# Trainium2, one core: a lightning indexer emitted in portions of half a projection, each held on TensorE behind that half

## The chip, the cores and the metric

The kernel runs on one core of a Trainium2 chip. The time is device microseconds of one execution, and the figure compared is the median of several executions. TensorE is called PE below, VectorE DVE, ScalarE ACT, GpSimd POOL, and SyncE, which issues the DMAs here, SP.

## What is computed

Two layers of a decoder trunk over 1024 tokens of width 1024, all in float32. Each layer normalises its input, multiplies it with one wide matrix, and runs two branches over the result: a sparse attention, whose keys are picked by an indexer, and a gated DeltaNet. The two branches are gated, added and multiplied with an output matrix. What matters here is the indexer and the choice of keys:

```python
raw = jnp.einsum('bqhd,bsd->bqhs', qib, k_idx)              # 8 index heads of width 64
iscore = jnp.einsum('bqhs,bqh->bqs', jax.nn.relu(raw), wb)  # one score per query and key
iscore = jnp.where(causal[None], iscore, -jnp.inf)
_, sel = lax.top_k(iscore, topk)                            # topk = 256 keys per query
```

Tokens come in eight blocks of 128 (`t` = 0 to 7). Blocks 0 and 1 see at most 256 keys, so only the blocks 2 to 7 (`SEL`) need scores and a choice.

## The kernel before, in words

Products in full precision are made of three matmuls: each operand is split into a high part (written by ACT, line 139) and a low part (DVE, line 140). A **projection** is 8 steps of k with three matmuls each, 24 in all, of 512 columns; `proj_tokens` (line 338) makes one per token block, `proj_feat` (line 361) one per half of 512 tokens.

A layer runs through `token_phase`, `feature_phase` and `attention`. The change is in `token_phase`. There the PE makes, in this order: the projections of the index columns (`first`, `second`); 24 projections of queries, keys and values (three chunks `ch` of eight blocks each); and 16 projections of the attention gates (`gate_a`, four features of four projections). With those 40 projections it shares its time with a generator, `self.beside`. This generator first gives the indexer (`index_scores`), and then the choice of keys (`select`, in two stages that alternate). After each projection `tick()` takes pieces out of the generator until their costs have used up `SHARE` = 4.0. What a piece emits stands in program order behind that projection. The framework's scheduler then makes a fixed queue for each engine, with program order as priority and with waits where data are needed; an instruction that it takes for ready may move ahead of one that isn't.

One **unit** of the indexer is a pair of index heads of one block: 6 or 12 matmuls of 64 rows (line 511) into the four banks `wide`, their relu on ACT (line 513) and two weighted additions into `scores` on DVE (lines 518 and 520). A unit costs `2 * n / S`, where n is the block's number of keys: 0.75 for block 2 up to 2.0 for block 7. There are four units per block, 24 in a layer. A block's queries are turned just ahead of its first unit: four PE transposes (line 498), then a split by ACT and DVE into `qi_hi` and `qi_lo`. Line 523 masks a block's finished scores.

`select` searches the 256th largest score of each query bit by bit: 31 iterations in each stage, one piece of cost `SEL_COST` = 1.5 each. Stage 0 has the blocks 5 (counted on DVE, line 544) and 4, 3, 2 (counted on ACT with Sign, line 562); stage 1 has block 7 on DVE and block 6 on ACT. Both stages share one buffer for DVE's count (`t_junk`) and one for ACT's (`t_junk2`), so their pieces follow each other. After the search come two corrective counts, and then a mask for each of six blocks (lines 607 to 613), which SP writes out (line 614).

When the phase ends its tiles are freed, and `feature_phase` takes their space: `xp` (line 682), `xf` (line 644) and the decay rows `H` (line 665). Projections of the first DeltaNet head can run ahead of that, since their results wait in PSUM; `acc` has two banks and `more` one, so three of them fit. Lines 687 and 688 move them into `xp` and `kf`.

SP holds one queue in order: the loads of weights (`w_raw`, line 303), the writing of masks (line 614), of staged tokens (line 387) and of gates (line 636) all pass through it.

Of the kernel before, what the change touches and what calls it, by code (L numbers as in the profile page):

```python
# [37 lines left out]
S = 1024  # L38
D = 1024
T = S // P  # L40
KT = D // P
# [13 lines left out]
SEL = list(range(TOPK // P, T))  # L55

SEL_STAGES = [([5], [4, 3, 2]), ([7], [6])]

SHARE, SEL_COST = 4.0, 1.5

GATES = (4, 2, 1, 1)

# [24 lines left out]
class Trunk:  # L87
    def __init__(self, ctx, tc, args):
        self.tc, self.nc = tc, tc.nc
        (self.x, self.positions, self.norm_gain, self.w_in, self.conv_w, self.a_log, self.dt_bias,  # L90
         self.gdn_gain, self.idx_gain, self.w_out, self.final_gain, self.out) = args
        self.depth = self.w_in.shape[0]
        self.const = ctx.enter_context(tc.tile_pool(name="const", bufs=1))
        self.dram = ctx.enter_context(tc.tile_pool(name="scratch", bufs=1, space=DRAM))
        self.act = ctx.enter_context(tc.tile_pool(name="act", bufs=1))
        self.small = ctx.enter_context(tc.tile_pool(name="small", bufs=2))
        self.wp = ctx.enter_context(tc.tile_pool(name="bulk", bufs=1))
        self.tags, self.turn = {}, 0
        self.beside = None
        ctx.enter_context(self.banks(acc=(1, 2), tr=(1, 2)))  # L100


# [178 lines left out]
                self.split(ht[0][:, ks, ts], ht[1][:, ks, ts], pt.rearrange("p (k t) -> p k t", k=4))  # L281
        return ht

    def tick(self):

        left = SHARE
        while left > 0 and self.beside is not None:
            cost = next(self.beside, None)
            if cost is None:
                self.beside = None  # L290
            else:
                left -= cost


    def w_tiles(self, srcs, n):
# [28 lines left out]
    def proj_tokens(self, weights, act, evac, t0=0, tag=lambda t: "acc", then=None):  # L324


        nc = self.nc
        ws, n, _ = weights
        order = [(t, k) for t in range(t0, T) for k in range(KT)]
        if then:  # L330
            order.sort(key=lambda x: (x[0], x[1]) if x[0] < T - 2 else (T - 2, x[1] + LAG * (x[0] == T - 1)))
        acc = {}
        for t, k in order:
            if t not in acc:
                acc[t] = self.bank(tag(t))
            ts = slice(t * P, (t + 1) * P)
            for i, (a, b) in enumerate(((act[0], 0), (act[0], 1), (act[1], 0))):
                nc.tensor.matmul(acc[t][:, :n], a[:, k, ts], ws[k][b][:, :n], start=k == 0 and i == 0,  # L338
                                 stop=k == KT - 1 and i == 2)
            if then and t == T - 1:  # L340
                then[0].append(next(then[2]))
            if k == KT - 1:
                evac(t, acc.pop(t)[:, :n])
                self.tick()

    def feat_weights(self, w, c0):

# [6 lines left out]
    def proj_feat(self, ws, half, act, evac, tag="acc"):  # L354

        hs = slice(half * 512, half * 512 + 512)
        acc = self.bank(tag)
        for k in range(KT):
            cs = slice((k % 4) * P, (k % 4 + 1) * P)
            for i, (a, b) in enumerate(((0, 0), (0, 1), (1, 0))):  # L360
                self.nc.tensor.matmul(acc, ws[k // 4][a][:, cs], act[b][:, k, hs], start=k == 0 and i == 0,  # L361
                                      stop=k == KT - 1 and i == 2)
        evac(hs, acc)
        self.tick()


    def token_phase(self, l, ip, ht, first):
# [92 lines left out]
    def index_scores(self, l, p, raw, scores):  # L460
        nc = self.nc
        shape = [P, T, 8]
        wi = self.small.tile(shape, F32, name="w_idx", bufs=1)
        nc.vector.tensor_scalar(wi, raw[:, :, 576:584], IDXH ** -0.5 * IDXD ** -0.5, None, op0=OP.mult)

        kn2 = p.tile([P, T, 2, IDXD], F32, name="relu", bufs=3)
        kn = kn2[:, :, 0]
        sq = p.tile([P, T, IDXD], F32, name="relu", bufs=3)
        kr = raw[:, :, 512:576]
        nc.vector.tensor_mul(sq, kr, kr)  # L470
        ssq = self.small.tile([P, T], F32, name="k_ssq")
        nc.vector.tensor_reduce(ssq, sq, axis=AX.X, op=OP.add)
        nc.vector.tensor_scalar(ssq, ssq, 1.0 / IDXD, EPS, op0=OP.mult, op1=OP.add)
        r = self.rsqrt(ssq, T)
        kshape = [P, T, IDXD]
        nc.vector.tensor_mul(kn, kr, r[:, :, None].to_broadcast(kshape))
        nc.vector.tensor_mul(kn, kn, self.ig[l][:, None, :].to_broadcast(kshape))
        self.rope(p, kn2[:, :, 0:1], slice(0, T), self.rope_i, 1)
        nc.scalar.copy(kn2[:, :, 1], kn)
        kh = p.tile([P, S], F32R, name="k_hi")  # L480
        kl = p.tile([P, S], F32R, name="k_lo")
        for half in range(2):
            pt = self.tr()
            for i in range(4):
                nc.tensor.transpose(pt[:, i * P:(i + 1) * P], kn2[:, 4 * half + i].rearrange("p a d -> p (a d)"),
                                    self.ident)
            hs = slice(512 * half, 512 * half + 512)
            self.split(kh[:, hs], kl[:, hs], pt)

        t0 = SEL[0]  # L490
        q4 = raw[:, t0:, 0:512].rearrange("p t (h d) -> p t h d", d=IDXD)
        self.rope(p, q4, slice(t0, T), self.rope_i, IDXH)
        for t in SEL:

            qh, ql = (p.tile([P, IDXH // 2, P], F32R, name=nm, bufs=2) for nm in ("qi_hi", "qi_lo"))
            pt = self.tr()
            for i in range(IDXH // 2):
                nc.tensor.transpose(pt[:, i * P:(i + 1) * P], raw[:, t, i * P:(i + 1) * P], self.ident)
            self.split(*(a.rearrange("p h t -> p (h t)") for a in (qh, ql)), pt)
            n = (t + 1) * P  # L500
            sc = scores[t]
            parts = 1 if n <= 512 else 2
            w = n // parts
            for i in range(IDXH // 2):
                rel = [p.tile([P, S], F32, name="relu", bufs=3) for _ in range(2)]
                for o in range(0, n, w):
                    ps = [self.bank("wide") for _ in range(2)]
                    for j, (a, b) in enumerate(((qh, kh), (qh, kl), (ql, kh))):
                        for half in range(2):
                            rows = slice(IDXD * half, IDXD * half + IDXD)  # L510
                            nc.tensor.matmul(ps[half][:, :w], a[rows, i], b[rows, o:o + w], start=j == 0, stop=j == 2)
                    for half in range(2):
                        nc.scalar.activation(rel[half][:, o:o + w], ps[half][:, :w], AF.Relu)
                for half in range(2):
                    h = 2 * i + half
                    wc = wi[:, t, h:h + 1]
                    if h == 0:
                        nc.vector.tensor_scalar(sc[:, :n], rel[half][:, :n], wc, 0.0, op0=OP.mult, op1=OP.add)
                    else:
                        nc.vector.scalar_tensor_tensor(sc[:, :n], rel[half][:, :n], wc, sc[:, :n], op0=OP.mult,  # L520
                                                       op1=OP.add)
                yield 2 * n / S
            nc.vector.tensor_tensor(sc[:, n - P:n], sc[:, n - P:n], self.causal_sel, op=OP.min)


# [620 lines left out]
```

## Time and profile before

| | us |
|---|---|
| median of three executions | 2730.17 (2725.91 to 2731.36) |
| the profiled execution, its own time | 2725.06 |
| its span from the first to the last instruction | 2723.3 |
| its mean granted TensorE clock | 0.976 of 2.4 GHz |

The profile is of one execution. Its span is 1.8 us shorter than its time, and its time lies 5.1 us under the median. "Busy" counts the time in which an engine worked on instructions. Behind each idle time stands the instruction that ended last before the engine could go on. The two layers run the same instructions: the index units stand at 86 to 168 us in the first layer and at 1432 to 1514 us in the second.

### The profile page before, as it was taken

How to read it: one execution, taken by the hardware profiler on the slowest of the kernel's cores; microseconds unless marked ns; L12 is line 12 of the kernel's file. 1: busy time of each engine (PE TensorE's matmuls, PEld its weight loads, DVE VectorE, ACT ScalarE, POOL GpSimd, SP SyncE). 2: the span in 40 equal slices, each digit the busy share in tenths (PEclk: the TensorE clock that was granted, in tenths of full speed). 3: DMA queues.
4: the chain of work that ended last, by engine and by line, in shares of the span. 5: the costliest groups of instructions: out<-in, count | busy, mean ns of one | idle time of the engine just before them, and what ended most of it. 6: DMA issues, size and time to landing. Idle time of an engine off the chain costs nothing.

```text
span 2723.3 us, 42939 instructions
## 1 busy us (share of the span) xinstructions
PE 2570.7 (94%) x14854; PEld 2140.5 (79%) x14854; DVE 1972.8 (72%) x5450; ACT 1316.8 (48%) x3169; POOL 111.9 (4%) x398
## 2 busy tenths in 40 slices
PE   7999989999999999999999999898999999999998
PEld 7677778777777888898786777686887778888986
DVE  6677967767787775697366888677676777757965
ACT  5579643343333332697245894433333343227962
POOL 0122000000000000000001210000000000000000
PEclk9999999999999999999999999998899999999999
DMA  3113332222222221531420232321212221226324
GB/s 121 48 66 90 85 87 56 49 51 57 61 51 53 50 73 51 174 105 35 157 65 30 78 101 71 77 63 47 53 42 65 51 57 46 69 63 180 92 68 143
DMA packets 283262, 202.95 MB, mean 75 GB/s; under 512 B 55906, under 2 KB 241188, under 8 KB 283044
## 3 DMA queue, kind: packets, MB, share of 16 engines
q1 hardware_dynamic: 283044, 200.20, 26.2%
q8 instruction: 117, 1.92, 0.3%
q14 instruction: 101, 0.83, 0.1%
HBM read 153.80 MB, written 46.33 MB: 73 GB/s over the span
## 4 chain that ended last, share of the span: by engine, by line
PE 68%; DVE 13%; ACT 7%; DMA 6%; issue 5%; POOL 1%; SPq 0%; DVEq 0%; POOLq 0%; ACTq 0%
PE acc L361 20%; PE acc L338 11%; PE more L361 9%; PE acc L1038 4%; PE wide L1006 4%; PE tr L758 2%; PE tr L1029 2%; ACT t_junk L562 2%; PE out L338 2%; ACT g_junk L723 2%; DMA w_raw<-in_w_in_dram 2%; DVE t_junk L544 2%; DVE w_lo L140 2%; DMA H<-rows 2%; PE tr L708 1%
## 5 line engine op out<-in xcount | busy, mean ns | idle before, releaser
L361 PE MATMUL acc<-hi_t,w_hi 128*128 128x512 f32 x1240 | 502.2, 405 | 8.3 <-DVE gate L629 7.3
L361 PE MATMUL acc<-hi_t,w_lo 128*128 128x512 f32 x1240 | 501.9, 405 | 0.0
L361 PE MATMUL acc<-lo_t,w_hi 128*128 128x512 f32 x1240 | 499.6, 403 | 0.0
L139 ACT CAST w_hi<-w_raw 128x512 fp32r<-128x512 f32 (+1 forms) x336 | 201.1, 602 | 371.0 <-PE acc L361 196.8
L140 DVE TENSOR_TENSOR w_lo<-w_raw,w_hi 128x512 fp32r<-128x512 f32 (+1 forms) x336 | 223.3, 668 | 149.2 <-ACT w_hi L139 136.0
L338 PE MATMUL acc<-w_hi,hi_t 128*128 128x512 f32 (+1 forms) x768 | 285.7, 373 | 12.6 <-ACT w_hi L139 7.3
L338 PE MATMUL acc<-w_lo,hi_t 128*128 128x512 f32 (+1 forms) x768 | 284.5, 371 | 2.1 <-DVE w_lo L140 1.9
L338 PE MATMUL acc<-w_hi,lo_t 128*128 128x512 f32 (+1 forms) x768 | 283.6, 369 | 0.0
L361 PEld LDWEIGHTS acc<-hi_t,w_hi 128*128 128x128 f32 x1240 | 236.7, 191 | 49.8 <-DVE gate L629 8.6
L361 PEld LDWEIGHTS acc<-hi_t,w_lo 128*128 128x128 f32 x1240 | 236.2, 190 | 41.1
L361 PEld LDWEIGHTS acc<-lo_t,w_hi 128*128 128x128 f32 x1240 | 236.3, 191 | 40.9
L562 ACT ACTIVATE t_junk<-scores,t_bits 128x640 f16<-128x640 f32 x248 | 198.8, 802 | 30.8 <-DVE t_bits L554 26.0
L361 PE MATMUL more<-hi_t,w_hi 128*128 128x512 f32 x488 | 198.8, 407 | 4.5 <-ACT kf L688 4.5
L361 PE MATMUL more<-hi_t,w_lo 128*128 128x512 f32 x488 | 199.2, 408 | 0.0
L361 PE MATMUL more<-lo_t,w_hi 128*128 128x512 f32 x488 | 198.3, 406 | 0.0
L338 PEld LDWEIGHTS acc<-w_hi,hi_t 128*128 128x128 f32 x768 | 146.2, 191 | 40.6 <-ACT w_hi L139 10.5
L338 PEld LDWEIGHTS acc<-w_lo,hi_t 128*128 128x128 f32 x768 | 146.7, 191 | 27.4 <-DVE w_lo L140 5.1
L338 PEld LDWEIGHTS acc<-w_hi,lo_t 128*128 128x128 f32 x768 | 146.6, 191 | 22.0 <-issue 1.0
L544 DVE TENSOR_SCALAR_CACHE_REDUCE t_junk<-scores,t_bits 128x1024 f16<-128x1024 f32 (+4 forms) x136 | 153.4, 1128 | 4.3
L849 DVE TENSOR_TENSOR xc<-xc,xtmp 128x248 f32<-128x248 f32 (+30 forms) x496 | 141.8, 286 | 3.1
L847 DVE TENSOR_TENSOR xtmp<-wide,xc 128x248 f32<-128x248 f32 (+30 forms) x496 | 141.6, 285 | 2.7
L806 ACT ACTIVATE o_junk<-vb 128x128 f32<-128x128 f32 x128 | 39.6, 310 | 162.3 <-DVE vb L803 126.3
(344 smaller groups left out, 5478.4 us busy)
## 6 DMA issues: line engine op xcount, KB each, us to landing
w_raw<-in_w_in_dram SPq DMA_DIRECT2D x272, 256.0 KB
qs<-stage SPq DMA_DIRECT2D x32, 256.0 KB
ya_gate<-gate SPq DMA_DIRECT2D x32, 256.0 KB
H<-rows SPq DMA_DIRECT2D x16, 512.0 KB
wide<-hscr SPq DMA_DIRECT2D x64, 128.0 KB
yb<-gate SPq DMA_DIRECT2D x32, 256.0 KB
w_raw<-in_w_out_dram SPq DMA_DIRECT2D x32, 256.0 KB
qraw<-qs SPq DMA_DIRECT2D x32, 256.0 KB
```

Source lines behind the costliest of these rows:

```text
L139: self.nc.scalar.copy(hi, src)
L140: self.nc.vector.tensor_sub(lo, src, hi.bitcast(F32))
L338: nc.tensor.matmul(acc[t][:, :n], a[:, k, ts], ws[k][b][:, :n], start=k == 0 and i == 0, stop=k == KT - 1 and i == 2)
L361: self.nc.tensor.matmul(acc, ws[k // 4][a][:, cs], act[b][:, k, hs], start=k == 0 and i == 0, stop=k == KT - 1 and i == 2)
L544: nc.vector.tensor_scalar(junk[:, :sc[i].shape[1]], sc[i], thr, 0.0, op0=op, op1=OP.add, accum_out=cnt[:, i:i + 1])
L562: nc.scalar.activation(junk[:, :n], sc[i], AF.Sign, bias=f(bits, i), scale=-1.0, accum_out=cnt[:, i:i + 1])
L723: nc.scalar.activation(junk, pt[:, c * P:(c + 1) * P], AF.Square, accum_out=ssq[:, col:col + 1])
L758: nc.tensor.matmul(pg[:, o0:o0 + P], kf[:, cs], a[:, cs], start=True, stop=True)
L847: nc.vector.tensor_mul(tmp[:, :, j + 1:], ln[:, None, j, j + 1:].to_broadcast(shape), X[:, :, j:j + 1].to_broadcast(shape))
L849: nc.vector.tensor_add(X[:, :, j + 1:], X[:, :, j + 1:], tmp[:, :, j + 1:])
L1006: nc.tensor.matmul(ps[:, :w], qt[a][:, i], kt[b][:, g, o:o + w], start=j == 0, stop=j == 2)
L1038: nc.tensor.matmul(po, a, b[:, cs], start=j == 0 and i == 0, stop=j == t and i == 2)
```

## The change

`tick` takes the matmul behind which the new work has to stand (`mm`), and is called twice in each projection, after the fourth and after the eighth step of k (`proj_feat` likewise). A call adds `SHARE` = 2.0 to a credit that is carried from call to call, and takes pieces while the credit is above zero. What is emitted stands inside `issue_after(mm.ins)`: an instruction on PE may not move ahead of that matmul. Other engines are not held. The cost of a unit is multiplied by `SCORE_COST` = 1.5, the preparation of the keys with the first queries becomes a piece of cost 1.5 of its own, and a piece of `select` costs 1.4 in place of 1.5. The queries of the next block are turned behind the second unit of a block, so two units ahead of their use; the first block's are turned in the piece of the preparation.

```diff
-SHARE, SEL_COST = 4.0, 1.5
+SHARE, SCORE_COST, SEL_COST = 2.0, 1.5, 1.4
...
-    def tick(self):
-
-        left = SHARE
-        while left > 0 and self.beside is not None:
-            cost = next(self.beside, None)
-            if cost is None:
-                self.beside = None
-            else:
-                left -= cost
+    def tick(self, mm):
+
+        if self.beside is None:
+            return
+        self.credit += SHARE
+        with self.tc.issue_after(mm.ins):
+            while self.credit > 0 and self.beside is not None:
+                cost = next(self.beside, None)
+                if cost is None:
+                    self.beside, self.credit = None, 0.0
+                else:
+                    self.credit -= cost
...
             if k == KT - 1:
                 evac(t, acc.pop(t)[:, :n])
-                self.tick()
+            if k % 4 == 3:
+                self.tick(mm)
...
+            if k == KT // 2 - 1:
+                self.tick(mm)
         evac(hs, acc)
-        self.tick()
+        self.tick(mm)
...
-        for t in SEL:
+
+        def queries(t):
...
             self.split(*(a.rearrange("p h t -> p (h t)") for a in (qh, ql)), pt)
+            return qh, ql
+
+        later = queries(t0)
+        yield SCORE_COST
+        for t in SEL:
+            qh, ql = later
...
-                yield 2 * n / S
+                if i == 1 and t + 1 < T:
+                    later = queries(t + 1)
+                yield SCORE_COST * 2 * n / S
```

## Rows read from the trace of the kernel before

**Rows 1.** The page: busy us, share of the span and instructions of each engine.
```profile
PE 2570.7 (94%) x14854; PEld 2140.5 (79%) x14854; DVE 1972.8 (72%) x5450; ACT 1316.8 (48%) x3169; POOL 111.9 (4%) x398
```
**Rows 2.** Waits of PE, 83 to 168 us: us, times, longest; last row 1429 to 1514.
```profile
PE wide L511 <- ACT qi_hi L139: 3.9, 4, 2.7
PE wide L511 <- ACT relu L513: 1.1, 3, 0.5
PE wide L511 <- DVE qi_lo L140: 0.7, 2, 0.4
...
PE wide L511 <- ACT qi_hi L139: 3.6, 4, 2.3
```
**Rows 3.** Hand-over: timeline of ACT and PE at 374 us, then in the second layer.
```profile
374.47 0.59 ACT L687 COPY xp<-acc 128x512 f32<-128x512 f32 x1 [4.81 <-DMA mask<-t_junk]
375.70 0.50 PE L361 MATMUL acc<-hi_t,w_hi 128*128 128x512 f32 x1 [1.04 <-ACT kf L688]
...
1721.06 0.58 ACT L687 COPY xp<-more 128x512 f32<-128x512 f32 x1 [7.13 <-DMA mask<-t_junk]
1722.29 0.50 PE L361 MATMUL more<-hi_t,w_hi 128*128 128x512 f32 x1 [3.35 <-ACT kf L688]
```
**Rows 4.** Line 361 alone: stretch and length, PE busy (count), PEld, clock, DMA, GB/s.
```profile
265.30:374.70 109.40, 105.70 (x456) 86.38 (x455) 0.98 0.33 92
```
**Rows 5.** Timeline of DVE (first row) and ACT about the search's start.
```profile
173.36 0.41 DVE L523 TENSOR_TENSOR scores<-scores,causal_sel 128x128 f32<-128x128 f32 x1
...
137.39 0.61 ACT L562 ACTIVATE t_junk<-scores,t_bits 128x384 f16<-128x384 f32 x1
...
177.68 1.04 ACT L562 ACTIVATE t_junk<-scores,t_bits 128x896 f16<-128x896 f32 x1 [6.58 <-DVE t_bits L554]
```
**Rows 6.** Stretches: length, PE busy, PEld, DVE, ACT, POOL (counts), clock, DMA, GB/s.
```profile
83.20:167.60 84.40, 78.21 (x433) 55.92 (x431) 53.63 (x78) 48.48 (x104) 13.04 (x42) 0.98 0.13 44
177.70:313.00 135.30, 130.72 (x561) 107.06 (x560) 113.20 (x342) 128.42 (x290) 25.31 (x96) 0.97 0.29 85
313.00:374.50 61.50, 57.84 (x247) 46.85 (x245) 50.54 (x109) 10.63 (x19) 0.00 (x0) 0.97 0.27 78
```
**Rows 7.** Line 511 on PE in each layer: minimum/median/maximum ns, first and last start.
```profile
L511 PEld LDWEIGHTS wide<-k_hi,qi_hi x80: 182/183/328, 86.6 to 166.6; 64*128 64x128 f32 x80
...
L511 PEld LDWEIGHTS wide<-k_hi,qi_hi x80: 182/183/326, 1432.8 to 1512.6; 64*128 64x128 f32 x80
```
**Rows 8.** Line 338 alone in three stretches; columns as in rows 4.
```profile
76.80:83.30 6.50, 5.99 (x24) 4.35 (x24) 1.00 0.55 137
...
83.30:167.50 84.20, 39.49 (x160) 29.01 (x159) 0.98 0.13 43
167.60:204.50 36.90, 36.90 (x162) 30.25 (x162) 1.00 0.19 65
```
**Rows 9.** A group of ACT, 177.68 to 313 us: count, busy, mean ns, idle before.
```profile
L562 ACT ACTIVATE t_junk<-scores,t_bits 128x896 f16<-128x896 f32 (+1 forms) x121 | 97.3, 804 | 8.9 <-DVE t_bits L554 6.6
```
**Rows 10.** Groups of DVE, 313 to 374.5 us; a second gate group equals the one shown.
```profile
L140 DVE TENSOR_TENSOR w_lo<-w_raw,w_hi 128x512 fp32r<-128x512 f32 x10 | 6.8, 681 | 0.0
...
L607 DVE TENSOR_SCALAR t_junk<-scores,t_bits 128x768 f16<-128x768 f32 (+5 forms) x6 | 3.5, 586 | 9.1 <-DMA mask<-t_junk 9.1
L629 DVE SCALAR_TENSOR_TENSOR gate<-th,acc 128x512 f32<-128x512 f32 x4 | 2.7, 680 | 0.0
```
**Rows 11.** Timeline of PE after a long wait.
```profile
405.24 1.11 PE L708 MATMUL tr<-ident,qf 128*128 128x128 f32 x4 [7.27 <-DVE kdec L713]
...
409.42 0.64 PE L361 MATMUL acc<-hi_t,w_hi 128*128 128x512 f32 x1
409.90 0.40 PE L361 MATMUL acc<-lo_t,w_hi 128*128 128x512 f32 x1
```
**Rows 12.** Timeline of ACT and PE where a load of weights came late.
```profile
332.24 0.62 ACT L139 CAST w_hi<-w_raw 128x512 fp32r<-128x512 f32 x1 [3.81 <-DMA w_raw<-in_w_in_dram]
...
334.35 0.53 PE L361 MATMUL acc<-hi_t,w_hi 128*128 128x512 f32 x1 [3.63 <-DVE gate L629]
```

More of the change, by code (lines that the diff above doesn't have):

```diff
@@ L282, in make_h @@
         return ht
-    def tick(self):
-        left = SHARE
-        while left > 0 and self.beside is not None:
-            cost = next(self.beside, None)
-            if cost is None:
-                self.beside = None
-            else:
-                left -= cost
+    def tick(self, mm):
[6 more added lines that the diff above has]
+                if cost is None:
+                    self.beside, self.credit = None, 0.0
+                else:
+                    self.credit -= cost
     def w_tiles(self, srcs, n):
@@ L337, in proj_tokens @@
             for i, (a, b) in enumerate(((act[0], 0), (act[0], 1), (act[1], 0))):
-                nc.tensor.matmul(acc[t][:, :n], a[:, k, ts], ws[k][b][:, :n], start=k == 0 and i == 0,
-                                 stop=k == KT - 1 and i == 2)
+                mm = nc.tensor.matmul(acc[t][:, :n], a[:, k, ts], ws[k][b][:, :n], start=k == 0 and i == 0,
+                                      stop=k == KT - 1 and i == 2)
             if then and t == T - 1:
@@ L360, in proj_feat @@
             for i, (a, b) in enumerate(((0, 0), (0, 1), (1, 0))):
-                self.nc.tensor.matmul(acc, ws[k // 4][a][:, cs], act[b][:, k, hs], start=k == 0 and i == 0,
-                                      stop=k == KT - 1 and i == 2)
+                mm = self.nc.tensor.matmul(acc, ws[k // 4][a][:, cs], act[b][:, k, hs], start=k == 0 and i == 0,
+                                           stop=k == KT - 1 and i == 2)
+            if k == KT // 2 - 1:
+                self.tick(mm)
         evac(hs, acc)
-        self.tick()
+        self.tick(mm)
     def token_phase(self, l, ip, ht, first):
```

## The prediction, made before the changed kernel was run

> **What bounds the kernel now.** I read the shares of the page first, then the waits of PE, then the places where PE waits, each in the view that shows who is late there. PE is busy 94% of the span [rows 1], so the first guess is that PE is the bound and that each wait taken from it shortens the kernel. In the stretch of the indexer these waits are small: 3.9 us on the split of the queries, 1.1 us on relu and 0.7 us on the low part, 5.7 us in the first layer; the second repeats the two small ones and has 3.6 us in the large, 5.4 us together [rows 2].
>
> The place that decides lies 207 us later. At 374.5 us ACT, idle for 4.81 us, starts on line 687 when the last mask has been written, because `xp` takes space that `select` held; PE goes on 1.2 us later, after 1.04 us of waiting. In the second layer the same pair waits 7.13 and 3.35 us [rows 3]. By then PE has made 456 matmuls of line 361, which is 19 projections: the 16 gates and the three that fit into free banks [rows 4]. So PE is out of work when the choice of keys ends, in both layers. From there back, the end of `select` sets the time, and PE has no slack to give.
>
> What sets the end of `select`? Its first Signs run at 134.8 to 138 us, one iteration of stage 0, and then none until 177.68 us [rows 5]: the stages alternate through shared buffers, so stage 0 cannot go on before stage 1 has begun, and stage 1 needs the scores of block 7, which line 523 finishes at 173.8 us. From 177.7 to 313 us ACT is busy 128.4 of 135.3 us: the search runs at ACT's pace. Then DVE makes masks for 61.5 us [rows 6]. The chain from the last index unit to the hand-over is stiff: its last group of matmuls starts at 166.6 and 1512.6 us [rows 7], `xp` at 374.47 and 1721.06 us, so 207.9 and 208.5 us, though PE waits 2.3 us longer in the second layer [rows 3].
>
> **The change part by part**, for one layer.
>
> *Where the last unit stands.* By the old costs the first tick gives five units, then 4, 4, 3, 3, 3 and 2: the 24th is out after seven projections. The seventh and eighth blocks of a chunk are made alternately (a lag of two steps of k), so five steps of the eighth stand ahead of it too: 7 x 24 + 15 = 183 matmuls. The trace shows 24 and 160 of line 338 up to there [rows 8], so the scheduler did follow program order. By the new costs a layer's indexer costs 1.5 + 1.5 x 33 = 51, and 2.0 come in per half projection. Adding it up piece by piece, the last unit comes out at the 25th call, after the first half of the 13th projection (block 4 of the second chunk): 300 matmuls. It cannot move ahead, because it is held. That is 117 matmuls of 36.9 / 162 = 0.228 us [rows 8] ahead of it that stood behind it: **+26.7 us** until the last scores. PE's total work is unchanged, but these projections no longer cover the search.
>
> *The waits of the indexer.* Queries turned two units ahead hide their split (on ACT and DVE) behind a whole unit and half a projection, and a unit per half projection gives ACT time for its relu. I let 5.5 us of 5.7 and 5.4 go [rows 2]: **-5.5 us**. Ends: -5.7, and -3 if the new spacing makes small waits of its own. If that cover were lost, the old waits would return and nothing more.
>
> *The backlog behind the last unit.* Before, the last call emits two units, and scores are finished 6 to 7 us after the last group starts (166.6 to 173.8 us) [rows 5, 7]. After it is one unit: **-2.2 us**, ends 0 and -2.6.
>
> *The search.* The 121 Signs in its stretch [rows 9] are the same, and PE makes about as many projections beside it, so ACT has about as many copies: **0**, ends -3 and +3. Emitting it at 1.4 moves its pieces behind later projections in program order, but it already ran later than emitted: the last iterations come out behind projection 29 of 40 before and 35 after, and by 313 us PE was at projection 32.
>
> *The masks.* In the 61.5 us DVE also does 10 splits (6.8 us) and 8 gate steps (twice 2.7 us), 12.2 us in all, some of it inside the 9.1 us for which it waits on the masks' DMAs [rows 10]. PE will be further ahead by then, with fewer evacuations left: **-4 us**, ends 0 and -12. The masks' DMAs move with them in SP's queue (a rival, below).
>
> *The restart.* PE will be idle for some 20 us where it waited 1 to 3. After 7.27 us idle its matmuls took 0.64 us until 409.9 us, then 0.40 [rows 11]: 4.7 us at what the durations show as the lower of its two clock levels (1.2 GHz), 2.3 us lost. Most of it falls into the next wait, that same 7.27 us: **+0.5 us**, ends 0 and +2.3.
>
> *At no cost.* The hold itself: units stood behind their projections before. On the ticks that carry only `select` it holds nothing, since `select` has no PE instruction. No unit issues a DMA.
>
> Sum: 26.7 - 5.5 - 2.2 + 0 - 4 + 0.5 = **+15.5 us per layer, +31 us for two**. Cross-check: PE's 207 us from the indexer's end to the hand-over lose 26.7 us of work, so PE arrives near 369 us or earlier, and the hand-over falls to about 390 us. The profiled execution took 2725.1 us, so 2756 us for its like; it lies 5.1 us under the median, and with the median of 2730.2 I say **2761 us**.
>
> **The rivals.**
>
> *Faster: PE is the bound after all.* The Trainium skill, "Perfetto Trace Analysis", § Identifying the Most-Contended Engine and § Optimization Strategy, says to optimise the engine with the highest occupancy first, and to close the gaps on it; the 94% of the profile's page agree with its choice of engine. As a mechanism here: spread over more projections the indexer leaves ACT free (35.9 of 84.4 us were free before [rows 6]), stage 0's Signs run there ahead of stage 1, the search ends no later than now, and only the 10.9 us of waits change: 2719 us. Three Signs of stage 0 at 0.804 us [rows 9] are 2.4 us per iteration, so the 15.5 us are won back with the seventh iteration run ahead; from there on it isn't slower. Against it stand the 40 us without a Sign [rows 5], and the code that makes the stages alternate is not changed. Chance 0.07.
>
> *Slower still: weights behind masks.* SP's queue is in order. Before, PE lost 3.63 us where a split waited 3.81 us on a late load [rows 12]. If the loads of the first head's weights come to stand behind masks that are now written later, the three projections that ran ahead run after the hand-over: 3 x 24 x 0.23 = 16.6 us per layer, 2761 + 33 = 2794 us. Against it: the loads ran between the masks before, and the three projections were done in time [rows 4]. Chance 0.09.
>
> *No change to speak of:* the change doesn't do what it says, because portions come out later but DVE and ACT take the gain and the loss in equal parts (waits -5.5 and masks -12, search -3, against 26.7 less the backlog): 2730 to 2737 us. Chance 0.04.
>
> **How the numbers follow.** Forecast 0.80, the three rivals 0.07, 0.09 and 0.04. The predicted time is 2761 us. All low ends at once give 26.7 - 5.7 - 2.6 - 3 - 12 = +3.4 us per layer (2737 us), all high ends 26.7 - 3 + 3 + 2.3 = +29 us (2788 us); neither is likely whole. I take 2742 to 2788 us. About 0.2% (5.5 us) is what a measurement can tell from no change: faster 0.07, the same 0.04, slower 0.89.
>
> **What would show it.** Right: the last group of line 511 starts some 19 to 21 us later after the indexer's start, with 300 projection matmuls ahead of it; the waits on `qi_hi` are gone; line 523 ends for block 7 near 192 us; ACT is full for about 135 us from there; and line 687 starts near 390 us with PE idle for some 20 us before it. Wrong, if Signs of stage 0 run in a row before block 7 has scores, if PE reaches line 687's wait with no idle time, or if the search takes clearly less than 135 us. PE idle ahead of the 19th projection with ACT waiting on `w_raw` would be the slower rival.

## The result and the profile after

| | before | after |
|---|---|---|
| median, us | 2728.86 (4 executions) | 2756.43 (4 executions, 2751.51 to 2757.67) |
| profiled execution: time, us | 2725.06 | 2756.95 |
| its span, us | 2723.3 | 2755.2 |
| mean granted TensorE clock | 0.976 | 0.969 |

The changed kernel takes 1.0098 of the time of the one before (95% interval 1.0081 to 1.0116), 27.6 us more. The forecast was +31 us. In the rows below some lines have moved: 338 is 341 now, 361 is 365, 511 is 524, 562 is 577, 607 is 622, 629 is 644, and 687 and 688 are 702 and 703.

The page's first row shows that every engine runs as many instructions as in [rows 1], and that PE is 12.8 us less busy, in a span that is 31.9 us longer:

```profile
PE 2557.9 (93%) x14854; PEld 2132.1 (77%) x14854; DVE 1973.9 (72%) x5450; ACT 1313.6 (48%) x3169; POOL 119.6 (4%) x398
```

The waits of PE, longest first (us in total, times, longest), show where the time is. Behind the first, which was 47.9 us before, stand two new ones, on the hand-over. The last row is the only wait of PE from 83 to 184 us: those of the indexer in [rows 2] are gone.

```profile
PE tr L840 <- DVE vb L836: 49.8, 10, 6.0
PE more L365 <- ACT kf L703: 35.5, 2, 33.9
PE acc L365 <- ACT kf L703: 31.8, 1, 31.8
...
PE tr L505 <- DVE idx_raw L259: 0.8, 1, 0.8
```

The hand-over itself, in the timelines of ACT and PE, first layer and second, answers to [rows 3]. ACT and PE both stand still until the last mask is written:

```profile
386.95 0.59 ACT L702 COPY xp<-acc 128x512 f32<-128x512 f32 x1 [35.53 <-DMA mask<-t_junk]
388.18 0.80 PE L365 MATMUL acc<-hi_t,w_hi 128*128 128x512 f32 x1 [31.75 <-ACT kf L703]
...
1751.85 0.59 ACT L702 COPY xp<-more 128x512 f32<-128x512 f32 x1 [37.66 <-DMA mask<-t_junk]
1753.08 0.79 PE L365 MATMUL more<-hi_t,w_hi 128*128 128x512 f32 x1 [33.88 <-ACT kf L703]
```

The stretches that answer to [rows 6] (length, then busy time and count of PE, PEld, DVE, ACT and POOL, granted clock, DMA share, GB/s): the indexer, the search, the masks. The indexer now runs with PE full and the clock at its upper level, and the search still takes 135 us at ACT's pace. In the masks' stretch PE has 28.7 us of work where it had 57.8, none of it behind 356.4 us, and the granted clock is 0.79, a mean over its two levels:

```profile
86.30:183.20 96.90, 96.77 (x531) 71.94 (x531) 55.74 (x78) 49.96 (x109) 24.38 (x67) 1.00 0.17 55
191.00:326.00 135.00, 131.27 (x575) 107.09 (x574) 118.01 (x351) 129.83 (x294) 17.50 (x66) 1.00 0.31 88
326.00:387.00 61.00, 28.70 (x126) 23.09 (x124) 45.54 (x100) 5.38 (x11) 0.01 (x1) 0.79 0.18 53
```

How far back the last unit stands is read from the projection's matmuls ahead of it: line 341 alone from the first projection to the last unit (columns as in rows 4; answers to [rows 8]), then the first and last start of line 524 in the two layers (answers to [rows 7]), and the first Sign behind the scores (answers to [rows 5]). It is 300 matmuls, and the last group starts 95.7 us after the first, where that was 80.0 us:

```profile
76.80:181.50 104.70, 74.22 (x300) 54.71 (x300) 1.00 0.20 61
...
L524 PEld LDWEIGHTS wide<-k_hi,qi_hi x80: 182/183/187, 86.4 to 182.1; 64*128 64x128 f32 x80
...
L524 PEld LDWEIGHTS wide<-k_hi,qi_hi x80: 182/183/187, 1450.3 to 1546.0; 64*128 64x128 f32 x80
...
190.99 1.04 ACT L577 ACTIVATE t_junk<-scores,t_bits 128x896 f16<-128x896 f32 x1 [4.24 <-DVE t_bits L569]
```

### The profile page after: what moved, and what is told of

The parts are those of the page before. It is cut to its first block, busy times and chain, and to the rows that moved or that the text cites. A ratio compares the mean times of both kernels' runs of the same rounds, so it can differ in the third digit from the quotient of the medians.

```text
span 2755.2 us, 42933 instructions
## 1 busy us (share of the span) xinstructions
PE 2557.9 (93%) x14854; PEld 2132.1 (77%) x14854; DVE 1973.9 (72%) x5450; ACT 1313.6 (48%) x3169; POOL 119.6 (4%) x398
## 4 chain that ended last, share of the span: by engine, by line
PE 68%; DVE 10%; ACT 8%; DMA 7%; issue 5%; SPq 1%; POOL 0%; DVEq 0%; ACTq 0%; POOLq 0%
PE acc L365 21%; PE acc L341 11%; PE more L365 9%; PE acc L1053 4%; PE wide L1021 4%; ACT t_junk L577 3%; PE tr L1044 2%; DMA H<-rows 2%; PE tr L773 2%; PE wide L524 2%; ACT g_junk L738 2%; PE out L341 2%; DMA w_raw<-in_w_in_dram 2%; DVE w_lo L140 1%; PE tr L723 1%
## 5 line engine op out<-in xcount | busy, mean ns | idle before, releaser
L365 PE MATMUL acc<-hi_t,w_hi 128*128 128x512 f32 x1240 | 501.9, 405 | 38.4 <-ACT kf L703 31.8
L577 ACT ACTIVATE t_junk<-scores,t_bits 128x640 f16<-128x640 f32 x248 | 198.6, 801 | 17.5 <-DVE t_bits L569 12.7
L341 PEld LDWEIGHTS acc<-w_lo,hi_t 128*128 128x128 f32 x768 | 145.3, 189 | 24.3 <-DVE w_lo L140 4.8
L341 PEld LDWEIGHTS acc<-w_hi,lo_t 128*128 128x128 f32 x768 | 145.3, 189 | 21.0
L365 PEld LDWEIGHTS more<-hi_t,w_hi 128*128 128x128 f32 x488 | 93.4, 191 | 51.4 <-ACT kf L703 36.3
```

The costliest lines, as they stand in the source:

```text
L341: mm = nc.tensor.matmul(acc[t][:, :n], a[:, k, ts], ws[k][b][:, :n], start=k == 0 and i == 0, stop=k == KT - 1 and i == 2)
L365: mm = self.nc.tensor.matmul(acc, ws[k // 4][a][:, cs], act[b][:, k, hs], start=k == 0 and i == 0, stop=k == KT - 1 and i == 2)
L577: nc.scalar.activation(junk[:, :n], sc[i], AF.Sign, bias=f(bits, i), scale=-1.0, accum_out=cnt[:, i:i + 1])
```

## The experiments

The theory is that of the prediction: the end of `select` sets the time, it hangs on the last unit of the indexer by a stiff chain, and the new pace puts that unit later. The rivals are that PE is the bound, or that the hold, the half portions or the early queries cost the time themselves. Each ratio is to the kernel before, measured beside it.

### The pace alone

```diff
-SHARE, SCORE_COST, SEL_COST = 2.0, 1.5, 1.4
+SHARE, SCORE_COST, SEL_COST = 2.0, 1.0, 1.4
```

> The changed kernel with a unit's cost multiplied by 1.0 in place of 1.5; hold, half portions and early queries stay. The last unit then comes out at the 17th call, behind 204 projection matmuls in place of 300: 96 x 0.228 = 21.9 us earlier per layer. Theory (the end of the choice of keys sets the time, and it hangs on the last unit): about 2756 - 44 = 2712 us, with PE's idle time ahead of xp down from about 32 to about 10 us per layer. Rival (the portions of half a projection or the hold cost the time): no way back, 2750 us or more.

Measured: 2711.55 us, ratio 0.9945 (0.9925 to 0.9965). The last group of units starts 74.4 us after the first, and PE's wait at the hand-over is 7.51 us. First the row of line 524, then those of ACT and PE:

```profile
L524 PEld LDWEIGHTS wide<-k_hi,qi_hi x80: 182/183/187, 86.8 to 161.2; 64*128 64x128 f32 x80
...
368.15 0.58 ACT L702 COPY xp<-acc 128x512 f32<-128x512 f32 x1 [11.29 <-DMA mask<-t_junk]
369.38 0.79 PE L365 MATMUL acc<-hi_t,w_hi 128*128 128x512 f32 x1 [7.51 <-ACT kf L703]
```

One constant turns the loss of 1% into a gain of 0.55%, with hold, half portions and early queries left in place. These three are not what costs; the pace is. The chain behind the last unit keeps its length: from its last group to the first copy into `xp` it is 368.15 - 161.2 = 207.0 us here, 204.9 us in the changed kernel and 207.9 us before, while PE's wait at its end is 7.5, 31.8 and 1.0 us.

### Without the hold

```diff
-        with self.tc.issue_after(mm.ins):
-            while self.credit > 0 and self.beside is not None:
+        while self.credit > 0 and self.beside is not None:
...
```

> The changed kernel without issue_after, all else the same. Theory: units follow program order without being held, so the last one stands behind about 300 matmuls as before, 2756 us within 4 us. Rival (the hold delays the indexer): units move ahead, and 10 us or more come back, 2745 us or less.

Measured: 2751.93 us, ratio 1.0101 (1.0083 to 1.0119), the same as the changed kernel's 1.0098. The units stand where they stood; line 523 here is the units' matmul:

```profile
L523 PEld LDWEIGHTS wide<-k_hi,qi_hi x80: 182/183/187, 85.7 to 181.4; 64*128 64x128 f32 x80
```

The hold does nothing here: program order had already put each unit behind its half.

### The early queries alone

```diff
-        for t in SEL:
+        def queries(t):
...
+            return qh, ql
+
+        later = queries(t0)
+        for t in SEL:
+            qh, ql = later
...
+                if i == 1 and t + 1 < T:
+                    later = queries(t + 1)
                 yield 2 * n / S
```

> The kernel before with nothing but the queries turned two units ahead; old ticks and costs. Theory: the waits on the split go (about 4.5 us per layer), the last unit comes as much earlier and so does the end of the choice: about 2729 - 9 = 2720 us; waits on relu inside the bursts stay. Rival (turning them early was what cost time): 2729 us or more.

Measured: 2727.30 us, ratio 1.0008 (0.9997 to 1.0019): neither the gain of 9 us nor a loss. The waits on `qi_hi` went, but waits on relu took their place, and the last unit did not come earlier: its last group starts 83.6 us after the first (first row), where that was 80.0 us. In the timeline of PE a unit waits 3.52 us for banks that relu has to empty (line 518 here), and in that of ACT Signs of the first iteration and a copy, which its queue has ahead of relu, run just then:

```profile
L516 PEld LDWEIGHTS wide<-k_hi,qi_hi x80: 182/183/327, 86.3 to 169.9; 64*128 64x128 f32 x80
...
139.36 0.74 PE L516 MATMUL wide<-k_hi,qi_hi 64*128 64x448 f32 x1 [3.52 <-ACT relu L518]
...
136.77 0.83 ACT L569 ACTIVATE t_junk<-scores,t_bits 128x640 f16<-128x640 f32 x1 [6.24 <-DVE t_bits L561]
...
137.60 0.56 ACT L381 COPY stage<-acc 128x512 f32<-128x512 f32 x1
138.06 0.72 ACT L569 ACTIVATE t_junk<-scores,t_bits 128x512 f16<-128x512 f32 x1
...
138.78 1.83 ACT L518 ACTIVATE relu<-wide 128x448 f32<-128x448 f32 x4
```

### Whole projections at the faster pace

```diff
-SHARE, SCORE_COST, SEL_COST = 2.0, 1.5, 1.4
+SHARE, SCORE_COST, SEL_COST = 4.0, 1.0, 1.4
...
-            if k % 4 == 3:
+            if k == KT - 1:
                 self.tick(mm)
...
-            if k == KT // 2 - 1:
-                self.tick(mm)
```

> The changed kernel with one call per whole projection (SHARE 4.0, credit carried, hold and early queries stay) and a unit's cost multiplied by 1.0: the same pace as e1_score100, but two to four units in a row. The last unit comes out behind nine projections, 216 matmuls in place of 204: 2.7 us later per layer. Theory (units in a row make PE wait for relu inside them, so the half portions are what frees PE): a further 2 to 5 us per layer, 2720 to 2727 us. Rival (half portions do nothing, only the place of the last unit counts): 2711.6 + 5.4 = 2717 us.

Measured: 2729.19 us, ratio 1.0012 (1.0003 to 1.0022), 17.6 us more than with half portions and a little above the range of the theory. The last unit stands behind 216 matmuls, 2.7 us of work more than in the first experiment, but its last group starts 83.5 us after the first, 9.1 us later. The rest, 6.4 us, is the units' own: line 522 here covers 35.06 us of PE, where the half portions needed 31.16 us (line 524), and PE idles 2.7 us more for relu. The rows are those lines alone, the wait, everything from 141.9 to 145.3 us, the first and last group, and the hand-over; the last row, by itself, is that of the half portions:

```profile
80.00:190.00 110.00, 35.06 (x240) 22.58 (x240) 0.98 0.17 53
PE wide L522 <- ACT relu L524: 2.7, 2, 2.4
141.90:145.30 3.40, 3.40 (x13) 2.27 (x11) 3.30 (x4) 2.47 (x6) 0.00 (x0) 0.50 0.20 77
...
L522 PEld LDWEIGHTS wide<-k_hi,qi_hi x80: 182/183/284, 86.4 to 169.9; 64*128 64x128 f32 x80
...
375.05 0.58 ACT L700 COPY xp<-acc 128x512 f32<-128x512 f32 x1 [12.74 <-DMA mask<-t_junk]
```
```profile
86.70:162.30 75.60, 31.16 (x240) 21.11 (x240) 1.00 0.14 46
```

So the half portions are worth 6.4 us per layer at the last unit. Not all of that is waiting for relu: 1 us behind PE's wait of 2.4 us the granted clock fell to its lower level (0.50) for the 3.4 us shown, which accounts for at most half of them, 1.7 us. Most of the 9.1 us reaches the hand-over: line 700 starts 375.05 - 86.4 = 288.7 us after the first unit, where it is 368.15 - 86.8 = 281.4 us with half portions, 7.3 us less. The rest of the 17.6 us was not traced.

### Ten iterations of the search left out, in both kernels

```diff
-        for b in range(30, -1, -1):
+        for b in range(30, 9, -1):
```

> The changed kernel with 21 of the 31 iterations of the search (the last ten bits are left out, so the chosen keys are not exact). Ten iterations of both stages are about 43 us of ACT per layer. Theory (the change takes time from PE, but the end of the choice sets the time): PE's idle 32 and 34 us ahead of xp go, about 2756 - 66 = 2690 us, up to 2705 us if another wait of the hand-over comes up. Rival (the change costs PE or ACT time of its own): still some 28 us behind the kernel before with the same cut.

> The kernel before with the same 21 of 31 iterations. Theory: PE idles only 1.0 and 3.4 us for the end of the choice, so the shorter search gives back about 5 us: 2720 to 2725 us, that is slower than the changed kernel with the same cut. Rival: falls as far as the changed one does, and stays ahead of it.

Measured: the changed kernel 2687.92 us, ratio 0.9866 (0.9845 to 0.9887); the one before 2724.97 us, ratio 0.9997 (0.9985 to 1.0009). The order is reversed, by 37 us. The kernel before gives back 1 us, which is not clear of noise, where about 5 us were expected. In the cut changed kernel PE waits 2.33 us at the hand-over; in the cut kernel before ACT waits for PE there, in both layers, and no longer for a mask (timelines of PE and of ACT):

```profile
363.32 0.50 PE L365 MATMUL acc<-hi_t,w_hi 128*128 128x512 f32 x1 [2.33 <-ACT kf L703]
```
```profile
375.54 0.59 ACT L687 COPY xp<-acc 128x512 f32<-128x512 f32 x1 [4.55 <-PE acc L361]
...
1721.07 0.59 ACT L687 COPY xp<-more 128x512 f32<-128x512 f32 x1 [4.55 <-PE more L361]
```

This is the sharpest of the runs. Before, PE and the end of `select` came to the hand-over almost together. The change makes PE some 18 us earlier (in the first layer it runs out of work at 388.18 - 31.75 = 356.4 us, before at 375.70 - 1.04 = 374.7 us [rows 3]) and the end of `select` some 13 us later, and only the later of the two counts.

### The masks' buffer

```diff
-            msk = p.tile([P, S], BF16, name="t_junk", bufs=1)
+            msk = p.tile([P, S], BF16, name="t_junk2", bufs=1)
```

> The changed kernel with the finished mask written into ACT's junk buffer, free by then, in place of the one in which the next block's comparison starts: DVE's five waits on the masks' DMAs between the blocks (3.7, 3.5, 1.9, 2.0 and 1.8 us, 12.9 in all in the first layer) go. Theory (the masks are on the path that sets the end): 2 x 12.9 us less, about 2730 us. Rival (PE sets the end): no change.

Measured: 2727.02 us, ratio 1.0005 (0.9995 to 1.0015): by the medians 29.4 us, by the ratios some 25 us less than the changed kernel. DVE's waits on the masks' DMAs are gone, and ACT's line 702 starts 14.1 us earlier than at 386.95 us. The group of DVE, then the row of ACT:

```profile
L622 DVE TENSOR_SCALAR t_junk<-scores,t_bits 128x768 f16<-128x768 f32 (+5 forms) x6 | 3.5, 582 | 0.0
372.89 0.58 ACT L702 COPY xp<-acc 128x512 f32<-128x512 f32 x1 [22.15 <-DMA mask<-t_junk]
```

### The stages' buffers

```diff
-            junk = p.tile([P, S], F16, name="t_junk", bufs=1)
+            junk = p.tile([P, S], F16, name=("t_junk", "t_run")[which], bufs=1)
...
-                junk = p.tile([P, S], F16, name="t_junk2", bufs=1)
+                junk = p.tile([P, S], F16, name=("t_junk2", "relu")[which], bufs=(1, 3)[which])
```

> The changed kernel with junk buffers of its own for each stage of the search (stage 1 counts into a tile of the masks and one of the relu, both idle then). Theory (the shared buffers hold stage 0 back): Signs of stage 0 run ahead of the scores of block 7, at 2.4 us per iteration in some 19 us of ACT's free time, so the search ends 15 us or more earlier per layer: about 2720 us. Rival (the queue's order holds stage 0 back, whatever the buffers): Signs still start behind block 7's scores, 2756 us.

Measured: 2739.78 us, ratio 1.0057 (1.0042 to 1.0072): by the medians 16.7 us, by the ratios some 11 us less than the changed kernel. Ahead of block 7's scores 30 Signs of stage 0 ran, where the changed kernel runs 3 (the groups of ACT's line 577 from 145 us to the scores' end, this kernel's first):

```profile
L577 ACT ACTIVATE t_junk<-scores,t_bits x30: 615/722/831, 151.7 to 196.2; 128x640 f16<-128x640 f32 x10, 128x512 f16<-128x512 f32 x10, 128x384 f16<-128x384 f32 x10
...
379.28 0.59 ACT L702 COPY xp<-acc 128x512 f32<-128x512 f32 x1 [4.68 <-DMA mask<-t_junk]
```
```profile
L577 ACT ACTIVATE t_junk<-scores,t_bits x3: 618/723/829, 152.2 to 154.0; 128x640 f16<-128x640 f32 x1, 128x512 f16<-128x512 f32 x1, 128x384 f16<-128x384 f32 x1
```

So the shared buffers do hold stage 0 back. At least half of the expected gain is lost again: the early Signs stand ahead of the units' relu and delay the scores' end from 187.1 to 198.1 us.

### Faster still, and both edits together

The next kernel has 0.7 as `SCORE_COST`; two more have 1.0 and 0.85 together with the masks' buffer from above.

> The changed kernel with a unit's cost multiplied by 0.7. The last unit comes out at the 12th call, behind 144 matmuls: 156 x 0.228 = 35.5 us earlier per layer than in the changed kernel, which is more than the 32 to 34 us that PE idles there. Theory: from there PE is the bound, about 2756 - 66 = 2690 us, or up to 2705 us if the denser units make PE wait for relu again. Rival (PE was the bound all along): 2719 us or more.

> Both helpful edits together: a unit's cost multiplied by 1.0 (e1_score100) and the finished mask in a buffer of its own (e6_mask_own). xp comes about 13.5 us earlier than in e1_score100, which is more than the 7.5 and 6.3 us that PE idles there. Theory: about 14 us less than 2711.6, 2698 us, or up to 2712 us if the copies of the first head come to wait behind the decay rows on ACT, as with a cost of 0.7. Rival (the two gains do not add since PE is the bound from e1_score100 on): 2711 us.

> As b1_score100_mask with 0.85 in place of 1.0: the last unit some 7 us earlier still. Theory: PE is the bound by then, so no further gain over b1_score100_mask within 4 us; more than that only if the end of the choice still sets the time.

Measured: 2710.05 us with 0.7, ratio 0.9946 (0.9928 to 0.9965), which is no better than 1.0 and misses the 2690 to 2705 us of the theory. The last mask is out at 363.6 us, but of the three waiting projections ACT moves only one; the others stand behind the decay rows `H` in its queue, and PE waits 8.09 us for them. The loads of these rows (line 680) start behind the last mask too: SP waits for its write before it issues them. The rows are of the timelines of ACT and PE, then SP's wait and POOL's wait for the first load:

```profile
363.61 0.59 ACT L702 COPY xp<-acc 128x512 f32<-128x512 f32 x1 [10.91 <-DMA mask<-t_junk]
...
372.95 2.44 ACT L684 ACTIVATE H<-H,ngm 128x128 f32<-128x128 f32 x8 [7.14 <-POOL H L681]
377.60 2.44 ACT L684 ACTIVATE H<-H,ngm 128x128 f32<-128x128 f32 x8 [2.20 <-POOL H L681]
379.95 0.56 ACT L702 COPY xp<-acc 128x512 f32<-128x512 f32 x1
...
381.15 0.79 PE L365 MATMUL acc<-hi_t,w_hi 128*128 128x512 f32 x1 [8.09 <-ACT kf L703]
...
SPq L680 <- DMA mask<-t_junk: 1.3, 1, 1.3
...
371.83 1.09 POOL L681 TENSOR_SCALAR_AFFINE_SELECT H<-H 128x1024 f32<-128x1024 f32 x1 [7.44 <-DMA H<-rows]
```

With 1.0 and the masks' buffer: **2696.77 us, ratio 0.9887 (0.9871 to 0.9904)**, the fastest complete kernel here. With 0.85 and the masks' buffer: 2702.57 us, ratio 0.9908 (0.9893 to 0.9923). Beyond a pace of about 1.0 an earlier last unit gains nothing more. That the choice of keys no longer matters there is not shown: PE still waits at the hand-over, for copies behind decay rows that are loaded only when the last mask is out. Nor is it shown why 0.85 gives back 5.8 us; in its first layer PE goes on 284.2 us after the first unit, where it is 286.0 us with 1.0, so the loss lies behind the hand-over.

## Why the prediction was right, step by step

**The bound.** Right. PE's 94% pointed at PE, and its waits went as announced, yet the kernel became slower, because PE had no work left at the hand-over. The cut search shows it from both sides, and also how narrow it was: in the kernel before, a shorter search gains nothing, so the end of `select` set the time there by no more than the 1.0 and 3.4 us that PE waited [rows 3].

**Where the last unit stands.** Right to the matmul: 300 in the row above, 204 and 216 in the experiments, all as counted from the credits.

**The waits of the indexer.** The mechanism was right, but the term was half of what it should have been. From the first start of a unit to the last takes 95.7 us in place of 80.0, so 15.7 us more, and 26.7 - 15.7 = 11.0 us went, where 5.5 were let go. I had counted only the time in which PE stood idle. Units in a row also waited for relu inside the burst, between two matmuls whose recorded times still overlap, so PE looked busy. The same 240 matmuls of line 511 cover 36.80 us before and 30.27 us after, 6.5 us less. Not all of it is waiting: behind the longest wait on the split (2.7 us) the granted clock was at its lower level from 136.7 to 140.1 us, and the units fill that stretch, so at most half of it, 1.7 us, is the clock's. The rows are stretches of that line alone and the weight loads' waits on relu, which show the waiting directly, before first:

```profile
86.50:167.60 81.10, 36.80 (x240) 23.56 (x240) 0.98 0.12 40
136.71:140.12 3.41, 3.41 (x17) 2.82 (x19) 0.50 0.22 82
PEld wide L511 <- ACT relu L513: 7.7, 23, 0.8
```
```profile
86.30:183.20 96.90, 30.27 (x240) 20.45 (x240) 1.00 0.17 55
PEld wide L524 <- ACT relu L526: 0.9, 3, 0.4
```

Two signs came out early by it: the last group starts 15.7 us later, not 19 to 21, and block 7's scores are finished at 187.1 us, not near 192.

**The backlog.** Right: from the last unit's last start to the first Sign of the search it is 190.99 - 182.1 = 8.9 us, and before 177.68 - 166.6 = 11.1 us; -2.2 us.

**The search.** Right: 135.0 us in the stretch above, 135.3 in [rows 6].

**The masks.** The step that failed in kind: -4 us were expected, and the stretch takes 61.0 us in place of 61.5. DVE did have fewer evacuations in it (6 splits and 3 gate steps, where it had 10 and 8), but it waited 12.9 us on the masks' DMAs in place of 9.1 [rows 10], so most of the gain went there:

```profile
L140 DVE TENSOR_TENSOR w_lo<-w_raw,w_hi 128x512 fp32r<-128x512 f32 x6 | 4.1, 685 | 0.0
L622 DVE TENSOR_SCALAR t_junk<-scores,t_bits 128x768 f16<-128x768 f32 (+5 forms) x6 | 3.5, 586 | 12.9 <-DMA mask<-t_junk 12.9
```

The waits grew mainly because what used to fill them was gone. In DVE's timelines the five gaps from a finished mask to the next block's first comparison add up to 12.1 us before, and DVE idled 9.1 of them; after, they add up to 12.9 us, and it idled them all. So about 3 of the 12.2 us of evacuations had cost nothing before.

**The restart.** +0.5 us was put in. PE's first nine matmuls behind the hand-over do run at the lower clock, from 388.18 to 392.19 us: 4.0 us, where 0.228 us for each make 2.1. But ACT's next copy out of PE's banks (line 702 at 404.69 us, line 687 at 391.34 us before) waits for the decay rows that stand ahead of it in ACT's queue, so this loss does not show there.

**The sum.** From the first unit's start to line 702 it is 386.95 - 86.4 = 300.6 us, and before 374.47 - 86.6 = 287.9 us: +12.7 us; in the second layer 1751.85 - 1450.3 = 301.6 and 1721.06 - 1432.8 = 288.3 us: +13.3 us. Together +26 us, where +31 were forecast; the misses of the waits (-5.5) and of the masks (+3.5) partly cancel. The two profiles differ by 31.9 us. The other 6 us lie in stretches in which the same instructions run, 5.0 us of them between the first layer's hand-over and the second layer's first unit, and they stay unexplained; the medians differ by 27.6 us. That the profiles' difference comes within 1 us of the forecast is luck: per layer the sum was 2 to 3 us too high.

**The idle time.** 32 and 34 us, not some 20: PE came to the hand-over earlier than the 369 us that I gave. The rows are all engines from the first unit to PE's end of work, before first. For the same matmuls PE idles 5.6 us in place of 14.5 and is busy 264.4 us in place of 273.6, at a granted clock of 1.00 in place of 0.98. I had not counted the waits in the bursts and the clock. It cost nothing more, because the hand-over does not depend on it.

```profile
86.60:374.70 288.10, 273.63 (x1258) 215.44 (x1258) 225.93 (x541) 189.10 (x415) 40.07 (x139) 0.98 0.24 71
```
```profile
86.40:356.40 270.00, 264.41 (x1261) 208.56 (x1261) 206.88 (x516) 186.96 (x414) 43.64 (x139) 1.00 0.24 72
```

**The rivals.** PE as the bound fell with the cut search (the waits summed for it are 5.7 + 5.4 = 11.1 us, not 10.9). No change to speak of would have needed a search and masks some 15 us shorter; they take 135.0 and 61.0 us. The buffers that alternate the stages hold them back as the prediction said, and in the changed kernel they were as they had been. Weights behind masks did not show: the three projections were done by 356 us.

## What to carry to other kernels

Find the place where two chains meet, and compare when each arrives, before you count what a change frees on the busiest engine; time that is freed ahead of a meeting with no slack is only turned into a wait. When work is spread out to fill gaps, ask what hangs on its last piece, and count where that piece comes to stand. The useful part of such a change can be kept by choosing the pace apart from the portion: half portions with the old density, and a buffer for the masks, beat both kernels.

## What the runs showed of the hardware that was not expected

A matmul that waits for a bank between two others need not show as idle PE time: in one layer some 5 us of such waiting lay inside "busy" time (36.80 against 30.27 us for the same 240 matmuls, less at most 1.7 us for 3.4 us at the lower clock), and could be read only from the weight loads' waits (7.7 against 0.9 us on relu) and from the length of the group.
